# Weight buffers 128 bytes longer: all begin at the same address modulo 256 bytes

## The chip, the cores and the metric

One Trainium2 chip, one core of it. The metric is the device time of one execution in microseconds (us). The names used below for the engines are those of the profile: PE is TensorE's matmul, PEld its weight load, DVE VectorE, ACT ScalarE, POOL GpSimd, SP the queue that issues the weight transfers.

## The reference

A decoder trunk of two layers over 256 tokens of width 1024, in float32. Cut to what matters here:

```python
for l in range(DEPTH):                       # 2
    h = rms_norm(x, norm_mix_pre[l])
    proj = h @ w_in[l]                       # q, k, v, lru_x, lru_gate, glu, branch gates
    y_a = dilated_attention_mixer(q, k, v, cos, sin, w_o_attn[l])
    y_b = rg_lru_mixer(lru_x, lru_gate, ..., w_o_lru[l])
    y_c = conformer_conv_mixer(glu_in, ..., w_o_conv[l])
    merged = g0 * y_a + g1 * y_b + g2 * y_c  # g = sigmoid(gate_logits)
    x = x + rms_norm(merged @ w_out[l], norm_mix_post[l])
    h = rms_norm(x, norm_mlp_pre[l])
    u = square(relu(h @ w_mlp_up[l]))
    x = x + rms_norm(u @ w_mlp_down[l], norm_mlp_post[l])
```

## The kernel before

All weights come as a stream of 1 MB chunks (128 partitions x 2048 floats), 92 per layer, in an order written out by hand (`ORDER` and `chunk_plan`). `weights(l, name)` handles one chunk: SP loads it into `raw` (2 buffers), ACT casts it to a high part `whi` (fp32r), and DVE subtracts to get the low part `wlo`; both parts have 3 buffers, used in turn. A product of float32 accuracy is then three matmuls: high x high, high x low, low x high. A scheduler (`Sched`) fixes the order of each engine's instructions beforehand from costs by instruction size; it looks at the sizes of the reads and writes, not at the buffers' lengths.

There are two forms of chunk.

- In the *stationary* form (names lx, glu, lg, q, k, ga, gb, gc, ob, oa, oc, up) the weights are loaded into the array (PEld) and the activations `hh`/`hl` stream past, 256 columns a matmul. A chunk is 48 matmuls: 16 with `whi` (high and low activations in turn), 8 with `wlo`, and the same again. `up` comes in pairs of chunks, 96 matmuls.
- In the *moving* form (v, wo, ua, dn) the activations are loaded and the weights stream, 512 columns a matmul. A chunk is 24 matmuls: in each half 8 that take `whi` and `wlo` in turn, and then 4 with `whi` alone. `dn` comes in pairs, 48 matmuls. In the MLP the two kinds alternate: an `up` pair, a `dn` pair, and so on (the loop over `kb`).

Each of these matmuls has a weight load of its own, and PE goes from one to the next without a wait. What this text calls the *spacing* is the time from the start of one matmul to the start of the next.

The change is about where the buffers lie. A buffer of `whi` or `wlo` is `CHUNK + LINE // 4` floats long, 2080 x 4 = 8320 bytes in a partition, which is 32.5 x 256. The pool holds 2 x `raw` (8192 bytes each), 3 x `whi`, 3 x `wlo`, end to end. In the program of before, the first `whi` begins 128 bytes past a multiple of 256; so the three `whi` begin at 128, 0 and 128 modulo 256, and the three `wlo` at 0, 128 and 0. Of three chunks in a row two have high at 128 and low at 0, and the third the other way round (high at 0, low at 128). The `dn` and `up` chunks of the second layer go through them like this (1 and 2 are the buffers with high at 128, 3 is the one with high at 0):

```
dn pair (buffers)   up pair after it (buffers)
dn00 dn01 (3, 1)    up4  up5  (2, 3)
dn10 dn11 (1, 2)    up6  up7  (3, 1)
dn20 dn21 (2, 3)    up8  up9  (1, 2)
dn30 dn31 (3, 1)    up10 up11 (2, 3)      and so on, with period three
```

Reads of a stationary chunk begin 64 bytes into its buffer (`off = LINE // 8`), those of a moving chunk at its start (but v1 and v2). The activation buffers that these matmuls read begin at 128 modulo 256. One chunk of the first layer, `dn61`, is held in eight buffers of another pool (`HOLD`), all of which begin at 128. The LRU's own weights (`lwh`, `lwl`, whose matmuls are called psr and psi) also lie in that pool, without the 64 bytes.

Of the kernel before, what the change touches and what calls it, by code (L numbers as in the profile page):

```python
# [8 lines left out]
F32R = mybir.dt.float32r  # L9
# [4 lines left out]
P = 128  # L14
# [5 lines left out]
CHUNK = 2048  # L20
# [72 lines left out]
NHI = 3  # L93
# [10 lines left out]
LINE = 128  # L104
# [272 lines left out]
def trunk_kernel(ctx: ExitStack, tc: tile.TileContext, x_d, pos_d, w_d, lruw_d, par_d, gain_d, const_d, id_d, out_d):  # L377
    nc = tc.nc
    cp = ctx.enter_context(tc.tile_pool(name="cp", bufs=1))
    wp = ctx.enter_context(tc.tile_pool(name="wp", bufs=1))  # L380
    sp = ctx.enter_context(tc.tile_pool(name="sp", bufs=1))
    pp = ctx.enter_context(tc.tile_pool(name="pp", bufs=1, space=bass.MemoryType.PSUM))
    S = Sched()
# [4 lines left out]
    def slot(name, dt=F32, shape=(P, 2, T)):  # L388
        return S.buf(sp, shape, dt, "s2", name, NSLOT)
# [58 lines left out]
    def dma(eng, out, in_, nbytes):  # L448
        def fn():
            o = out.ap() if isinstance(out, View) else out  # L450
            i = in_.ap() if isinstance(in_, View) else in_
            eng.dma_start(out=o, in_=i)

        e = {id(nc.gpsimd): "POOL", id(nc.scalar): "ACT"}.get(id(eng), "SP")
        o = S.op(e, DMA_ISSUE[e], fn, views(in_), views(out))
        o.dma = nbytes / DMA_RATE / 1e3
        return o
# [40 lines left out]
    def split(hi, lo, src, scale=None):  # L498
        if scale is None:
            return act(hi, src, AF.Copy), tt(lo, src, hi.f32(), OP.subtract)  # L500
        return (act(hi, src, AF.Copy, scale=scale),
                stt(lo, src, scale, hi.f32(), OP.mult, OP.subtract))
# [5 lines left out]
    def weights(l, name, spread=False):  # L508
        c = CIDX[name]
        assert c == used[l], (name, c, used[l])  # L510
        used[l] += 1
        nm = f"{name}_{l}"
        raw = S.buf(wp, (P, CHUNK), F32, "raw", f"raw_{nm}", NRAW)
        if l or c:
            o = dma(nc.sync, raw.all(), w_d[l * NCH + c], CHUNK * P * 4)
            if l == 0 and c in late:
                S.follow(o, late[c])
        else:
            for s in range(2):
                o = dma(nc.sync, raw[:, s * HALF:(s + 1) * HALF], w_d[0][:, s * HALF:(s + 1) * HALF], HALF * P * 4)  # L520
                if ORDER[0][0] == "v":
                    S.follow(o, x1_load)
        if spread:
            hs, ls = [], []
            for q in range(4):
                hs.append(slot(f"whi_{nm}{q}", F32R, (P, 512)))
                ls.append(slot(f"wlo_{nm}{q}", F32R, (P, 512)))
                for o in split(hs[q].all(), ls[q].all(), raw[:, q * 512:(q + 1) * 512]):
                    o.prep = True
            return [(Quarters(hs[2 * s:2 * s + 2]), Quarters(ls[2 * s:2 * s + 2])) for s in range(2)]  # L530
        off = 0 if KIND[name] == "as" and name[:2] not in ("v1", "v2") else LINE // 8
        hi = Shifted(S.buf(wp, (P, CHUNK + LINE // 4), F32R, "whi", f"whi_{nm}", NHI), off)
        lo = Shifted(S.buf(wp, (P, CHUNK + LINE // 4), F32R, "wlo", f"wlo_{nm}", NHI), off)
        n = HALF if l == 0 and c < 2 else PREP
        for b in range(0, CHUNK, n):
            for o in split(hi[:, b:b + n], lo[:, b:b + n], raw[:, b:b + n]):
                o.prep = True
        return [(Part(hi, s * HALF), Part(lo, s * HALF)) for s in range(2)]
# [196 lines left out]
    for l in range(L):  # L735
# [49 lines left out]
        def glu(i):  # L785
            w = weights(l, f"glu{i}")
            ps = mm_ps(f"glu{i}_{l}")
            gemm(f"glu{i}", w, ps, hr)
            if i % 2 == 0:
                upad[i // 2] = S.buf(sp, (P, 2, 288), F32, "upad", f"upad{i}_{l}", 4)  # L790
                memset(upad[i // 2][:, :, 0:30], 0.0)
            u2 = upad[i // 2]
            th = slot(f"gth{i}_{l}", shape=(P, T))
            act(th.all(), ps[:, 1, :], AF.Tanh, scale=0.5)
            stt(u2[:, i % 2, 30:30 + T], th.all(), 1.0, ps[:, 0, :], OP.add, OP.mult)
            if i % 2 == 1:
                conv_pair(i // 2)
# [3 lines left out]
        def lx(j):  # L801
            w = weights(l, f"lx{j}")
            ps = mm_ps(f"lx{j}_{l}")
            gemm(f"lx{j}", w, ps, hr)
            xp = S.buf(sp, (P, 2, 260), F32, "xp", f"xp{j}_{l}", 2)
            memset(xp[:, :, 0:3], 0.0)
            act(xp[:, :, 3:3 + T], ps.all(), AF.Copy)
            u = slot(f"lu{j}_{l}")
            for s in range(2):
                i = 2 * j + s  # L810
                act(u[:, s, :], ps[:, s, :], AF.Identity, scale=p1(par, CW + 24 + i), bias=p1(par, CB + i))
            for k in range(3):
                for s in range(2):
                    i = 2 * j + s
                    stt(u[:, s, :], xp[:, s, k:k + T], p1(par, CW + k * 8 + i), u[:, s, :], OP.mult, OP.add)
            lu[j] = u
            luh[j] = slot(f"luh{j}_{l}", F32R)
            lul[j] = slot(f"lul{j}_{l}", F32R)
            split(luh[j].all(), lul[j].all(), u.all())
# [3 lines left out]
        def lg(j):  # L823
            w = weights(l, f"lg{j}")
            ps = mm_ps(f"lg{j}_{l}")
            gemm(f"lg{j}", w, ps, hr)
            q = slot(f"gq{j}_{l}")
            act(q.all(), ps.all(), AF.Square, scale=0.044715 ** 0.5)
            stt(q.all(), q.all(), 1.0, ps.all(), OP.add, OP.mult)
            act(q.all(), q.all(), AF.Tanh, scale=0.7978845608028654)  # L830
            g = slot(f"gel{j}_{l}")
            stt(g.all(), q.all(), 1.0, ps.all(), OP.add, OP.mult)
            gel[j] = g
# [319 lines left out]
        for t in range(2):  # L1153
            nm = f"pm{l}{t}"
# [79 lines left out]
        for t in range(2):  # L1234
            nm = f"pd{l}{t}"
# [100 lines left out]
```

## Time and profile before

| | us |
|---|---|
| three runs | 1129.45, 1129.23, 1126.79 (median 1129.23) |
| the profiled execution | 1128.12 |
| its span, first to last instruction | 1126.3 |
| PE busy in the span | 1101.3 |
| PEld busy | 1025.4 |
| DVE busy | 903.2 |
| ACT busy | 719.7 |

The profiled execution is the one that all rows are from. A row of the chain of waits is a stretch of the work that ended last: start, length, engine, and how many instructions in a row; length by count is the mean spacing. A row of the timeline has start, length, and the instruction; the difference of two starts is the spacing. The length of one matmul (0.28 or 0.39 us) contains its way through the array, overlaps with the next ones, and is not the spacing.

### The profile page before, as it was taken

How to read it: one execution, taken by the hardware profiler on the slowest of the kernel's cores; microseconds unless marked ns; L12 is line 12 of the kernel's file. 1: busy time of each engine (PE TensorE's matmuls, PEld its weight loads, DVE VectorE, ACT ScalarE, POOL GpSimd, SP SyncE). 2: the span in 40 equal slices, each digit the busy share in tenths (PEclk: the TensorE clock that was granted, in tenths of full speed). 3: DMA queues.
4: the chain of work that ended last, by engine and by line, in shares of the span. 5: the costliest groups of instructions: out<-in, count | busy, mean ns of one | idle time of the engine just before them, and what ended most of it. 6: DMA issues, size and time to landing. Idle time of an engine off the chain costs nothing.

```text
span 1126.3 us, 20586 instructions
## 1 busy us (share of the span) xinstructions
PE 1101.3 (98%) x8258; PEld 1025.4 (91%) x8258; DVE 903.2 (80%) x1374; ACT 719.7 (64%) x1173; POOL 76.4 (7%) x168
## 2 busy tenths in 40 slices
PE   7999999999999999999999999999999999999995
PEld 5999999999899899889889999999988988989984
DVE  6999999999879865555579999999995899555552
ACT  5879938687765554445569896569775756444441
POOL 1000022111000010000010000221200001000000
PEclk9999999999999999999999999999999999999998
DMA  8764366654345555555465643755624465555540
GB/s 290 246 207 151 147 229 221 212 179 134 149 170 190 201 209 189 190 184 190 182 225 187 207 159 141 252 191 197 205 96 163 153 239 189 192 184 189 199 174 38
DMA packets 37649, 209.76 MB, mean 186 GB/s; under 512 B 6449, under 2 KB 9777, under 8 KB 14130
## 3 DMA queue, kind: packets, MB, share of 16 engines
q1 hardware_dynamic: 32976, 200.05, 50.2%
q0 software_dynamic: 4576, 8.40, 2.3%
q8 instruction: 65, 1.06, 0.4%
q14 instruction: 30, 0.25, 0.1%
q10 hardware_dynamic: 2, 0.00, 0.0%
HBM read 201.08 MB, written 1.05 MB: 179 GB/s over the span
## 4 chain that ended last, share of the span: by engine, by line
PE 81%; DVE 7%; DMA 4%; ACT 4%; issue 1%; SPq 1%; POOL 0%; DVEq 0%; POOLq 0%; ACTq 0%
PE dn L476 15%; PE up L476 14%; PE glu L476 8%; PE v L476 5%; PE gc L476 4%; PE ga L476 4%; PE wo L476 4%; PE lx L476 4%; PE oc L476 4%; PE lg L476 4%; PE k L476 3%; PE ua L476 2%; PE oa L476 2%; PE ob L476 2%; PE pv L476 1%; PE tp L483 1%
## 5 line engine op out<-in xcount | busy, mean ns | idle before, releaser
L429 DVE TENSOR_TENSOR wlo_dn<-raw_dn,whi_dn 128x1024 fp32r<-128x1024 f32 (+1 forms) x66 | 75.8, 1189 | 68.6 <-ACT whi_dn L416 68.5
L416 ACT CAST whi_dn<-raw_dn 128x1024 fp32r<-128x1024 f32 (+1 forms) x66 | 64.4, 1022 | 75.8 <-PE dn L476 44.1
L433 DVE SCALAR_TENSOR_TENSOR c<-upad,parh,c 128x256 f32<-128x256 f32 x256 | 110.2, 476 | 0.1
L476 PE MATMUL up<-hh_mlp,whi_up 128*128 128x256 f32 x448 | 106.3, 278 | 0.0
L476 PE MATMUL up<-hl_mlp,whi_up 128*128 128x256 f32 x448 | 106.0, 278 | 0.0
L476 PE MATMUL dn<-wlo_dn,uh 128*128 128x512 f32 x256 | 100.5, 393 | 0.0
L476 PE MATMUL dn<-whi_dn,uh 128*128 128x512 f32 x256 | 100.4, 392 | 0.0
L429 DVE TENSOR_TENSOR wlo_up<-raw_up,whi_up 128x1024 fp32r<-128x1024 f32 x56 | 66.4, 1221 | 39.0 <-ACT whi_up L416 39.0
L423 ACT ACTIVATE cpd<-upad,parh 128x256 f32<-128x256 f32 x224 | 94.5, 500 | 4.1 <-DVE c L429 4.1
L476 PEld LDWEIGHTS up<-hl_mlp,whi_up 128*128 128x128 f32 x448 | 84.3, 188 | 0.6
L476 PEld LDWEIGHTS up<-hh_mlp,whi_up 128*128 128x128 f32 x448 | 84.2, 188 | 0.6
L416 ACT CAST whi_up<-raw_up 128x1024 fp32r<-128x1024 f32 x56 | 56.2, 1048 | 36.3 <-PE dn L476 20.0
L476 PE MATMUL dn<-whi_dn,ul 128*128 128x512 f32 x256 | 70.8, 392 | 0.0
L429 DVE TENSOR_TENSOR cpd<-cpd 128x1024 f32<-128x1024 f32 (+2 forms) x84 | 63.2, 772 | 0.9 <-ACT cpd L423 0.9
L476 PE MATMUL up<-hh_mlp,wlo_up 128*128 128x256 f32 x448 | 60.7, 278 | 0.0
L476 PE MATMUL glu<-hh_mix,whi_glu 128*128 128x256 f32 x256 | 59.6, 276 | 0.0
L476 PE MATMUL glu<-hl_mix,whi_glu 128*128 128x256 f32 x256 | 59.6, 276 | 0.0
L476 PEld LDWEIGHTS dn<-whi_dn,ul 128*128 128x128 f32 x256 | 48.0, 188 | 10.8
L476 PEld LDWEIGHTS dn<-wlo_dn,uh 128*128 128x128 f32 x256 | 48.0, 188 | 10.4
L476 PEld LDWEIGHTS dn<-whi_dn,uh 128*128 128x128 f32 x256 | 48.1, 188 | 10.3
L476 PEld LDWEIGHTS up<-hh_mlp,wlo_up 128*128 128x128 f32 x448 | 55.7, 188 | 0.0
L476 PEld LDWEIGHTS glu<-hh_mix,whi_glu 128*128 128x128 f32 x256 | 48.0, 188 | 0.0
(306 smaller groups left out, 3380.2 us busy)
## 6 DMA issues: line engine op xcount, KB each, us to landing
raw_dn<-w_in_stream SPq DMA_DIRECT2D x32, 1024.0 KB, 4.8
raw_up<-w_in_stream SPq DMA_DIRECT2D x28, 1024.0 KB, 4.8
raw_glu<-w_in_stream SPq DMA_DIRECT2D x16, 1024.0 KB, 4.9
raw_q<-w_in_stream SPq DMA_DIRECT2D x12, 1024.0 KB, 4.9
raw_k<-w_in_stream SPq DMA_DIRECT2D x12, 1024.0 KB, 4.8
raw_v<-w_in_stream SPq DMA_DIRECT2D x11, 1024.0 KB, 4.9
raw_lx<-w_in_stream SPq DMA_DIRECT2D x8, 1024.0 KB, 4.9
raw_lg<-w_in_stream SPq DMA_DIRECT2D x8, 1024.0 KB, 4.8
```

Of the source, the lines that this page charges most:

```text
L416: nc.scalar.copy(out.ap(), in_.ap())
L423: nc.scalar.activation(out.ap(), in_.ap(), func, scale=val(scale), **kw)
L429: lambda: nc.vector.tensor_tensor(out=out.ap(), in0=a.ap(), in1=b.ap(), op=op), [a, b], [out])
L433: lambda: nc.vector.scalar_tensor_tensor(out=out.ap(), in0=a.ap(), scalar=val(s), in1=b.ap(), op0=op0, op1=op1), [a, b] + views(s), [out])
L476: nc.tensor.matmul(out.ap(), lhsT=lhs.ap(), rhs=rhs.ap(), start=start, stop=stop)
L483: nc.tensor.transpose(out.ap(), a.ap(), ident.all().ap())
```

## The change

The two buffers become `CHUNK + LINE // 2` floats long, 2112 x 4 = 8448 bytes, which is 33 x 256. All three `whi` and all three `wlo` now begin at 128 modulo 256. What lies behind them in a partition moves by 6 x 128 = 768 bytes, three times 256. Instructions, their order, and the 64 bytes stay.

```diff
         off = 0 if KIND[name] == "as" and name[:2] not in ("v1", "v2") else LINE // 8
-        hi = Shifted(S.buf(wp, (P, CHUNK + LINE // 4), F32R, "whi", f"whi_{nm}", NHI), off)
-        lo = Shifted(S.buf(wp, (P, CHUNK + LINE // 4), F32R, "wlo", f"wlo_{nm}", NHI), off)
+        hi = Shifted(S.buf(wp, (P, CHUNK + LINE // 2), F32R, "whi", f"whi_{nm}", NHI), off)
+        lo = Shifted(S.buf(wp, (P, CHUNK + LINE // 2), F32R, "wlo", f"wlo_{nm}", NHI), off)
```

## Rows read from the trace of the kernel before

**Rows 1.** The page: span, PE, and the granted clock in 40 slices.

```profile
span 1126.3 us, 20586 instructions
...
PE 1101.3 (98%) x8258; PEld 1025.4 (91%) x8258; DVE 903.2 (80%) x1374; ACT 719.7 (64%) x1173; POOL 76.4 (7%) x168
...
PEclk9999999999999999999999999999999999999998
```

**Rows 2.** The chain of waits, MLP of the second layer: start, length, instructions.

```profile
959.80 11.06 PE dn L476 x48
970.86 10.90 PE up L476 x96
981.76 11.01 PE dn L476 x48
992.77 11.08 PE up L476 x96
...
1014.90 11.31 PE up L476 x96
...
1092.64 22.15 PE dn L476 x96
```

**Rows 3.** Timeline of PE, end of dn41 (buffer 2), up12 (buffer 3).

```profile
1057.67 0.39 PE L476 MATMUL dn<-whi_dn,uh 128*128 128x512 f32 x1
...
1058.13 1.07 PE L476 MATMUL dn<-whi_dn,ul 128*128 128x512 f32 x4
1059.03 0.28 PE L476 MATMUL up<-hh_mlp,whi_up 128*128 128x256 f32 x1
1059.15 0.28 PE L476 MATMUL up<-hl_mlp,whi_up 128*128 128x256 f32 x1
```

**Rows 4.** Timeline of PE, the held chunk dn61, second use.

```profile
554.10 0.39 PE L476 MATMUL dn<-whi_dn,uh 128*128 128x512 f32 x1
...
555.49 0.39 PE L476 MATMUL dn<-whi_dn,uh 128*128 128x512 f32 x1
...
556.85 0.40 PE L476 MATMUL dn<-whi_dn,uh 128*128 128x512 f32 x1
```

**Rows 5.** Timeline of PE, end of dn01 (buffer 1), up4 (buffer 2).

```profile
969.78 1.09 PE L476 MATMUL dn<-whi_dn,ul 128*128 128x512 f32 x4
970.70 0.28 PE L476 MATMUL up<-hh_mlp,whi_up 128*128 128x256 f32 x1
970.83 0.28 PE L476 MATMUL up<-hl_mlp,whi_up 128*128 128x256 f32 x1
970.94 0.28 PE L476 MATMUL up<-hh_mlp,whi_up 128*128 128x256 f32 x1
```

**Rows 6.** Timeline of PE, end of dn21 (buffer 3), up8 (buffer 1).

```profile
1013.82 1.09 PE L476 MATMUL dn<-whi_dn,ul 128*128 128x512 f32 x4
1014.74 0.28 PE L476 MATMUL up<-hh_mlp,whi_up 128*128 128x256 f32 x1
```

**Rows 7.** The chain of waits, both layers' lx, glu and lg.

```profile
30.83 27.20 PE glu L476 x240
...
63.47 16.32 PE glu L476 x144
79.79 10.88 PE lx L476 x96
94.99 10.88 PE lg L476 x96
107.31 10.27 PE lg L476 x88
...
647.19 11.31 PE lg L476 x96
```

**Rows 8.** Busy time by window, 117 to 201 us: each engine, clock, DMA.

```profile
117.00:201.00 84.00, 81.62 (x714) 80.40 (x714) 80.44 (x118) 57.23 (x94) 11.98 (x25) 1.00 0.58 198
```

**Rows 9.** The instructions that write wlo_up: duration ns min/median/max.

```profile
L429 DVE TENSOR_TENSOR wlo_up<-raw_up,whi_up x56: 1211/1220/1226, 387.5 to 1078.1; 128x1024 fp32r<-128x1024 f32 x56
```

## The prediction

> **What bounds the kernel now.** The page comes first: PE is busy 1101.3 of 1126.3 us, and its granted clock is at the upper level, 2.4 GHz, in practically every slice [rows 1]. So the time is a number of matmuls times their spacing, and the question is whether the spacing depends on where a buffer begins.
>
> The chain of waits answers that, because it counts matmuls in a row. 240 glu matmuls take 27.20 us, 113.3 ns each, and the second run of 144 has the same 113.3 [rows 7]. But `up`, with the same instructions on the same shapes, takes 10.90, 11.08 or 11.31 us for 96: 113.5, 115.4 and 117.8 ns [rows 2]. The first layer has the same three lengths for its `up` pairs, twice each, in another order. There are thus two spacings in the stationary form, a short one of 113.3 and a long one of 117.8, and 11.08 is a pair that changes from one to the other. `lg` shows both as well: 10.88 for 96 in the first layer, 11.31 in the second [rows 7]. Nobody waits in these stretches. The three lengths of `up` go with the three positions in the ring of buffers: buffers (2, 3) give 10.90, (3, 1) give 11.08, (1, 2) give 11.31. This is what the change touches.
>
> The moving form is finer. A `dn` pair takes 11.06 or 11.01 us for 48, 230.4 and 229.4 ns [rows 2]. Just before up12, two matmuls that take the high buffer at 128 and the low one at 0 last 0.46 us together, 230 ns each; then four in a row from the buffer at 128 last 0.90, about 226 each [rows 3]. In the held chunk, where everything begins at 128, the first six matmuls last 1.39 us, 231.7 each, and the next six 1.36, 226.7 [rows 4]: with all at 128 the spacing settles on its short value within six matmuls and stays.
>
> **The change part by part.**
>
> *Moving form (dn, wo).* After the change every weight read of dn and wo begins at 128, as in the held chunk. I take six matmuls at 231.7 and the rest at 226.7: a dn pair is then 6 x 0.2317 + 42 x 0.2267 = 10.91 us, against 11.06 (two pairs of three) and 11.01 (one of three). In a layer the six pairs dn0 to dn5 gain 4 x 0.15 + 2 x 0.10 = 0.80, and the last 96 matmuls go from 22.15 to 21.79, 0.36 [rows 2]. That is 1.16 for 384 matmuls, 3.0 ns each; with the 192 of wo at the same rate, 960 x 3.0 = 2.9 us less over both layers. Bounds: 0.2267 for all of them from the first matmul gives 3.3; if the spacing stays at 231.7, dn loses some 1.3 us. ua and the two v chunks of this form at 128 are cut up by transposes: nothing.
>
> *Stationary form: up.* Here all weight reads move to the offset that buffers 1 and 2 have for high parts now (128 + 64 = 192). Two things decide: with which spacing an `up` pair begins, and whether it changes on the way.
>
> For the second, a pair in buffers (1, 2) holds the long spacing over all 96 matmuls (11.31), though its reads alternate between offsets; the way back to the short one is seen only in pairs that use buffer 3, where the high part lies at 0 and the low one at 128 [rows 2]. After the change no buffer lies so. A long spacing will stay long, and a short one short.
>
> For the first, the end of the preceding dn pair matters. There are three cases now. After dn01, whose last four matmuls still have the slow spacing of 230 ns (0.92 for four), up4 has one spacing of 0.13 and is then short [rows 5]. After dn21 (last buffer with high at 0; 0.92 for four) up8 is long from the start [rows 6, 2]. After dn41 (last buffer with high at 128, dn settled at 226 ns) up12 is long from the first matmul on: 0.12 us [rows 3]. After the change every dn pair ends as dn41 does, settled at 226.7. What differs from up12 is only the offset of up's own reads, 192 in place of 64. The two offsets are alike once the spacing is short: glu goes through all three buffers at 113.3 [rows 7]. I therefore take the entry of up12: long.
>
> Then all twelve uninterrupted `up` pairs of both layers take 11.31. Now they sum to 4 x (10.90 + 11.08 + 11.31) = 133.16; 12 x 11.31 = 135.72. Cost: +2.6 us. The bound on the other side is the short spacing for all, 12 x 96 x 0.1133 = 130.5: -2.6. The first pair of each layer is interrupted by transposes and counts 0.
>
> *Stationary form: lx and glu.* They follow v0, a moving chunk, which will end settled like dn. Twelve chunks (240 + 144 + 96 matmuls of rows 7 and two more chunks of 48) run one after the other, 576 a layer, short now. Entered long and with no way back, they cost 576 x (117.8 - 113.3) = 2.6 us a layer, +5.2 in both. Bounds: 0 and 5.2.
>
> *lg.* It follows psr and psi. In the second layer lg enters buffers (1, 2) from them long (11.31), in the first layer buffer 3 short (10.88) [rows 7]. With all offsets as in (1, 2) I take it long: 10.88 to 11.31 and 10.27 to 88 x 0.1178 = 10.37, +0.5. The second layer is long already: 0. Bounds: -0.6 and +0.6.
>
> *From 117 to 201 us, and the same stretch of the second layer*: PE is busy 81.62 of 84.00 us [rows 8], the rest it waits for rotary and LRU work of DVE, ACT and their transfers. A change of spacing is covered by those 2.4 us: 0. Without that cover 14 chunks, 672 matmuls, would cost up to 3.0 a layer.
>
> *From 201 to 360 us* (ga, gc, k, oa, oc between score matmuls and transposes) both spacings occur and every interruption starts anew. I take 0; all long or all short is about 1.5 us a layer either way.
>
> *The writers.* DVE's subtraction into `wlo` takes 1211 to 1226 ns in all 56 chunks of `up`, which went through all three buffers [rows 9]. So the begin of a buffer costs the writers nothing, and no transfer moves: SP loads `raw`, which stays. The 768 bytes by which other pools move are three times 256; the trace shows no dependence on more than that, and I count 0.
>
> *Sum.* -2.9 + 2.6 + 5.2 + 0.5 = +5.4 us. The sum is made on the profiled execution, 1128.12 us; its median over three runs is 1.1 higher, 1129.23. That gives 1134.6 us.
>
> **A rule against it.** By the rows, PE's spacing differs by 4% between buffers while its clock, form and shape are the same [rows 2]. The Trainium skill, page "TensorE: Matmul & The Clock Gate", section "Step-by-step: what each phase is for", says that PE has two independent SBUF read ports, and that loading the next weights takes no read bandwidth from the running matmul. By that rule alone the addresses could not matter, and the change would give 1129.2; the trace disagrees already before the change, in 10.90 against 11.31 us.
>
> **The rivals.**
>
> *The short spacing on entry (faster).* Place: the first matmuls of up and lx after a settled moving chunk. Reads at 192 after a moving chunk from 128 are short within three matmuls after dn01 [rows 5]; the only long entry after a settled dn is at offset 64 [rows 3]. If 192 is what makes the difference, up is short in all pairs (-2.6), lx and glu stay as they are (0), dn and wo give -2.9, lg +0.5: -5.0, 1124.2 us. Against it: up8 at offset 192 enters long and holds it [rows 6, 2]. It decides as soon as the first `up` pair after a dn pair is below 10.95 us.
>
> *Nothing that can be measured.* Either the two spacings come from how the kinds of matmul follow one another and not from the addresses, so that the change does not do what it is about, and long stretches move about without a change of their share; or up turns long and dn short while glu keeps 113.3, which is -2.9 + 2.6 + 0.5 = +0.2. Then 1129.2 to 1129.4. For it: glu, lx and the first lg pair of the first layer keep 113.3 ns [rows 7] although they cross all three buffers. Against the first of these: up's lengths repeat with the period of the ring.
>
> **How the numbers follow.** A measurement here tells about 0.3% from no change, 3.4 us. Forecast (long entry, held): 0.50; its own range is 1131.5 to 1137.5, from glu long in one layer only to 201-360 us long as well. Faster rival: 0.27, 1122.5 to 1125.5. Nothing: 0.23. The range 1123.5 to 1137.5 leaves out the outer part of both, less than 2 in 10. Slower by over 0.3%: 0.49; within: 0.25; faster: 0.26.
>
> **What will show it.** In the chain of waits: dn pairs at 10.9 us for 48 (step one); all up pairs of one length, 11.31 if the entry is long, 10.88 if it is short (step two); 27.20 or 28.27 us for the 240 glu matmuls (step three); lg at 11.31 in both layers. The prediction fails if the long spacing finds a way back with all reads at one offset, or if a settled dn hands over short; it fails on dn if its pairs stay at 11.06.

## The result and the profile after

The changed kernel takes 1134.72 us, median of four runs (1134.37 to 1136.28); the kernel before, run beside it, 1128.64. The ratio is 1.0052, interval 1.0031 to 1.0073: slower by 3.5 to 8.2 us, with 1134.6 forecast. The profiled execution of the changed kernel took 1134.92 us, its span 1133.2: 6.9 more than before.

The page after, to be held against [rows 1]:

```profile
span 1133.2 us, 20586 instructions
...
PE 1112.2 (98%) x8258; PEld 1040.2 (92%) x8258; DVE 904.4 (80%) x1374; ACT 720.8 (64%) x1173; POOL 76.2 (7%) x168
...
PEclk9999999999999999999999999999999999999998
```

The same 8258 matmuls, the same granted clock, but PE is busy 10.9 us longer (and its weight loads 14.8); DVE and ACT gain about 1 us each. The time in which PE does nothing falls from 25.0 to 21.0 us, so PE does not wait longer; its matmuls stand further apart, and a part of that fills what were waits. Where, the chain of waits of the changed kernel says (start, length, instructions in a row), against [rows 2] and [rows 7]:

```profile
24.40 5.66 PE lx L476 x48
30.05 28.27 PE glu L476 x240
...
63.98 16.96 PE glu L476 x144
...
341.61 22.61 PE oc L476 x192
...
364.23 20.43 PE wo L476 x90
...
399.21 2.83 PE up L476 x24
402.48 8.18 PE up L476 x72
...
652.90 11.31 PE lg L476 x96
...
798.60 11.31 PE k L476 x96
...
898.33 21.76 PE oc L476 x192
...
966.52 10.90 PE dn L476 x48
977.42 11.31 PE up L476 x96
...
1099.80 21.80 PE dn L476 x96
```

Read as spacings: 240 glu matmuls at 28.27 us are 117.8 ns (113.3 before), the 144 at 16.96 the same; each of the twelve uninterrupted `up` pairs takes 11.31; each `dn` pair 10.90 or 10.91, 227 ns. The three lengths of `up` and the two of `dn` have become one each.

Two of these rows show that 192 is not the long spacing by itself. oc takes 22.61 us in the first layer and 21.76 in the second, 117.8 and 113.3 ns, with all its reads at 192 both times. And the first `up` pair, which transposes interrupt, is long in its first 24 matmuls (2.83 us) and short in the 72 behind the transposes (8.18).

### The profile page after: what moved, and what is told of

Read it like the earlier page. It is cut to its first block, busy times and chain, and to the rows that moved or that the text cites. A ratio compares the mean times of both kernels' runs of the same rounds, so it can differ in the third digit from the quotient of the medians.

```text
span 1133.2 us, 20586 instructions
## 1 busy us (share of the span) xinstructions
PE 1112.2 (98%) x8258; PEld 1040.2 (92%) x8258; DVE 904.4 (80%) x1374; ACT 720.8 (64%) x1173; POOL 76.2 (7%) x168
## 4 chain that ended last, share of the span: by engine, by line
PE 92%; DMA 3%; ACT 1%; DVE 1%; SPq 1%; issue 1%; POOL 0%; DVEq 0%; POOLq 0%; ACTq 0%
PE dn L476 15%; PE up L476 14%; PE glu L476 8%; PE k L476 6%; PE v L476 5%; PE q L476 4%; PE gc L476 4%; PE ga L476 4%; PE lg L476 4%; PE lx L476 4%; PE oc L476 4%; PE wo L476 4%; PE gb L476 3%; PE ob L476 3%; PE oa L476 2%; PE ua L476 2%
## 5 line engine op out<-in xcount | busy, mean ns | idle before, releaser
L476 PEld LDWEIGHTS glu<-hl_mix,whi_glu 128*128 128x128 f32 x256 | 48.5, 189 | 0.0
```

Of the source, the lines that this page charges most:

```text
L476: nc.tensor.matmul(out.ap(), lhsT=lhs.ap(), rhs=rhs.ap(), start=start, stop=stop)
```

## The experiments

All are built on the program before or after; none leaves work out. A stationary read begins at the buffer's 128 plus four times the second pair of offsets, a moving read at 128 plus four times the first, modulo 256: an offset of 0 floats is 128, 16 is 192, 32 is 0, 48 is 64. "Moving" here means v0, wo, ua and `dn`; v1 and v2 follow the stationary offsets. The buffers of all but the first kernel have the changed length.

| stationary high, low | moving | us | ratio to before, 95% |
|---|---|---|---|
| as before, rest moved by 768 bytes | as before | 1128.7 | 0.9987 to 1.0011 |
| 192, 192 (the change) | 128 | 1134.72 | 1.0031 to 1.0073 |
| 192, 192 | alternating, as before | 1134.12 | 1.0030 to 1.0063 |
| alternating, as before | 128 | 1127.96 | 0.9981 to 1.0009 |
| 64, 192 | 128 | 1124.97 | 0.9942 to 0.9975 |
| 192, 64 | 128 | 1133.95 | 1.0028 to 1.0057 |
| 0, 0 | 128 | 1148.68 | 1.0158 to 1.0199 |
| 128, 128 | 128 | 1151.62 | 1.0183 to 1.0224 |
| 64, 64 | 0 | 1143.74 | 1.0096 to 1.0157 |
| 64, 192 | 192 | 1124.94 | 0.9951 to 0.9984 |
| 64, 192, order high, high, low | 128 | 1121.08 | 0.9910 to 0.9953 |
| 192, 192, same order | 128 | 1137.19 | 1.0053 to 1.0092 |
| 192, 64, same order | 128 | 1124.68 | 0.9951 to 0.9976 |

**Only the 768 bytes.**

```diff
+    memset(S.buf(sp, (P, 192), F32, "pad", "pad", 1, False)[:, 0:1], 0.0)
```

> The kernel before with one spare tile of 768 bytes ahead of the pool behind the weight buffers: all other tiles move as far as the change moved them, the weight buffers stay where they were. Mine (the weight reads' own begin modulo 256 sets the spacing): nothing moves; dn pairs of the second layer stay at 11.01 to 11.06 us, up pairs at 10.90, 11.08 and 11.31, glu at 27.20 for 240; 1128 to 1130 us. Rival (the 768 bytes by which everything else moved did it): up pairs all at 11.31, glu at 28.27; about 1134.7 us.

Measured 1128.7 us, and the chain has the old lengths:

```profile
972.67 10.89 PE up L476 x96
...
994.57 11.08 PE up L476 x96
...
1016.71 11.31 PE up L476 x96
```

The shift of the other pools is worth nothing: what acts is where the weight reads begin.

**The two halves of the change, one at a time.** First stationary reads all at 192 as in the change, with moving reads at the old alternation:

```diff
+        third = ring[0] % 3 == 2
+        ring[0] += 1
-        off = 0 if KIND[name] == "as" and name[:2] not in ("v1", "v2") else LINE // 8
+        off = ((32, 0) if third else (0, 32)) if KIND[name] == "as" and name[:2] not in ("v1", "v2") else (16, 16)
```

> The changed buffers, stationary reads all at 192 modulo 256 as in the change; but the moving reads alternate between 128 and 0 from chunk to chunk of the ring as they did before. Mine (it is the settled end of the moving chunk that makes the next stationary chunk long): dn pairs at 11.01 to 11.06 as before, glu at 27.20 for 240, up by its place in the ring, 10.90 where the dn before it does not settle and 11.31 where it does; about 1129.5 us. Rival (one constant offset of the stationary reads is by itself the long spacing): up 11.31 in all pairs, glu 28.27, and no gain on dn: about 1137.5 us.

Measured 1134.12: the time that I expected was missed by 4.6 us. The chain:

```profile
30.78 28.27 PE glu L476 x240
...
587.58 27.20 PE glu L476 x240
...
975.84 10.89 PE up L476 x96
986.73 11.01 PE dn L476 x48
997.74 11.31 PE up L476 x96
...
1020.11 11.31 PE up L476 x96
```

`dn` and `up` came with the ring's period, as I expected. But the pair at 1020.11 is long behind a `dn` pair that does not settle (its last chunk has high at 0), and glu was long in the first layer and short in the second, after a v0 that does not settle in either. After an unsettled moving chunk the entry can thus go both ways, and I had taken it for short. The rival falls too: reads at 192 throughout can be short (27.20, 10.89). What they lack is a way back, which the 11.31 behind the 11.01 shows: before, the pair at that place of the ring took 11.08 [rows 2]. Of the time, 2.5 us went into lx and glu of the first layer, about 1 into the two MLPs, and 1.6 into the stretch from ob (201.99 before, 204.55 now) to wo (360.76 and 364.88), which I had counted at nothing.

Then the other half, moving reads all at 128, stationary reads alternating as before (`third` as above):

```diff
+        off = (0, 0) if KIND[name] == "as" and name[:2] not in ("v1", "v2") else (48, 16) if third else (16, 48)
```

> The changed buffers, moving reads all at 128 modulo 256 as in the change; the stationary reads alternate as before (two chunks of three with high at 192 and low at 64, the third the other way round). Mine (the entry is long after every settled dn, and the third chunk's high at 64, low at 192 brings it back): dn 10.91, up about 10.95 to 11.1 where the pair contains the third chunk, 11.31 where it does not; glu back to short within its first three chunks, 27.2 to 27.6 for 240; about 1127 us. Rival (nothing brings a long spacing back once dn hands over settled): as the change, about 1134.7 us.

Measured 1127.96. The chain:

```profile
582.86 27.48 PE glu L476 x240
...
970.56 11.17 PE up L476 x96
...
992.63 11.08 PE up L476 x96
...
1014.62 11.31 PE up L476 x96
```

The moving chunks settle (10.90 to 10.94 us a `dn` pair), every pair enters long, and a chunk with high at 64 and low at 192 brings it back: in the second half of the pair (11.17), at the end of its first chunk (11.08), or not at all where the pair has no such chunk (11.31). What `dn` gains, `up` loses. By the medians the moving half is worth -0.7 us, within the interval of nothing, and the stationary half +5.5; the loss is the stationary half's, because it takes the way back away.

**High at 64, low at 192 in every buffer.**

```diff
+        off = (0, 0) if KIND[name] == "as" and name[:2] not in ("v1", "v2") else (48, 16)
```

> The changed buffers, but the reads of a stationary chunk begin at 64 modulo 256 in the high part and at 192 in the low part, in every buffer; moving reads at 128 as in the change. This is the one combination with which a long spacing went back to the short one before. Mine (a long spacing ends where high at 64 hands over to low at 192): dn stays at 10.91 a pair, each up pair enters long and is short again within its first chunk, 10.93 to 11.15 us, and holds that; glu 27.20 to 27.4 for 240; about 1125 us, faster than both kernels. Rival (after a settled dn the long spacing holds whatever the offsets of the stationary reads): up 11.31, glu 28.27, about 1134.7 us.

Measured 1124.97, 0.42% faster than before. The chain, and the timeline of PE in up4, behind a settled dn01:

```profile
24.72 5.63 PE lx L476 x48
30.36 27.20 PE glu L476 x240
...
970.83 11.08 PE up L476 x96
```

```profile
972.55 1.11 PE L476 MATMUL up<-hh_mlp,wlo_up 128*128 128x256 f32 x8
973.50 0.28 PE L476 MATMUL up<-hh_mlp,whi_up 128*128 128x256 f32 x1
...
975.38 1.09 PE L476 MATMUL up<-hh_mlp,wlo_up 128*128 128x256 f32 x8
976.30 0.28 PE L476 MATMUL up<-hh_mlp,whi_up 128*128 128x256 f32 x1
```

From the first row to the second are eight low matmuls in 0.95 us, still long; from the third to the fourth eight in 0.92, and all that follow are 113.3 apart. Each pair is long until its second handoff from high to low, some 41 matmuls, and then short. The first handoff does not do it here. It is no rule: the pairs of 11.17 us in the kernel before this one are 64 long matmuls and 32 short ones, and there the pair's first handoff from high at 64 to low at 192 ended it.

**The mirror image, 192 and 64.**

```diff
+        off = (0, 0) if KIND[name] == "as" and name[:2] not in ("v1", "v2") else (16, 48)
```

> The mirror image of the kernel with high at 64 and low at 192: high parts of stationary chunks are read at 192 modulo 256, low parts at 64, in every buffer; moving reads at 128. Mine (only a handoff from high at 64 to low at 192 ends a long spacing; the other direction does not): up pairs 11.31 us, glu 28.27 for 240, dn 10.91: about 1134.7 us, as the change. Rival (any change of offset between the high and the low part ends it): up 11.08, glu 27.20: about 1125 us, as with 64 and 192.

Measured 1133.95, and the chain stays long:

```profile
975.90 11.31 PE up L476 x96
```

All twelve pairs are like this one. In blocks of 16 high and 8 low, that a read changes its offset is not enough.

**Other constant offsets.** Stationary reads at 0, and then without the 64 bytes, at 128:

```diff
+        off = (0, 0) if KIND[name] == "as" and name[:2] not in ("v1", "v2") else (32, 32)
```

> The changed buffers, but every stationary read begins at 0 modulo 256, in the high and in the low part; moving reads at 128. Mine (one constant offset has no way back, whichever it is): up pairs 11.31, glu 28.27 for 240, about 1134.7 us. Rival (what matters is where the weight load begins in relation to the activations at 128: half of 256 apart they do not disturb each other): up 10.88, glu 27.20, about 1123 us.

```diff
+        off = (0, 0) if KIND[name] == "as" and name[:2] not in ("v1", "v2") else (0, 0)
```

> The changed buffers without the 64 bytes of the stationary chunks: every weight read, stationary and moving, begins at 128 modulo 256, as the activations do. Mine: a constant offset has no way back, and psr and psi, which read at 128 already, are spaced 120 ns in the trace; so up at 11.3 to 11.5 us a pair and glu at 28.3 to 28.8: 1135 to 1141 us. Rival (only reads at 64 or 192 are ever long): up 10.88, glu 27.20, about 1123 us.

Measured 1148.68 and 1151.62, far beyond both expectations. The chain at 0, then at 128:

```profile
31.01 28.80 PE glu L476 x240
...
335.71 11.39 PE oa L476 x96
...
990.66 11.53 PE up L476 x96
```

```profile
31.32 28.80 PE glu L476 x240
...
992.62 11.51 PE up L476 x96
```

28.80 us for 240 is 120.0 ns: a third spacing, and none shorter in the glu chunks and the uninterrupted `up` pairs. At 0 I had expected 117.8. The cost is not limited to these: at 128 every stationary chunk is at 120.0, and at 0 several others are at 118.7 (oa, 11.39 for 96). With 0, the stretch from ob to wo of the first layer alone grows by 3.9 us (201.99 to 360.76 before, 207.19 to 369.89 now), and I had priced only `up` and glu.

**All alike, but at 64 and 0.**

```diff
+        off = (32, 32) if KIND[name] == "as" and name[:2] not in ("v1", "v2") else (48, 48)
```

> All buffers alike as in the change, but at another place: moving reads all begin at 0 modulo 256, stationary ones all at 64. Mine (the moving form settles because its reads begin at 128, not because they are all alike): dn pairs stay at 11.0 to 11.1 us, up pairs enter as they may and hold what they enter with, 11.31 for most, glu 28.27 in at least one layer: 1134 to 1138 us. Rival (being alike is what settles it): dn 10.91, up 11.31, glu 28.27: about 1134.7 us; dn tells them apart, not the time.

Measured 1143.74; the time is 6 us above what I expected, and where they went was not traced, while `dn` decides as I expected:

```profile
973.88 11.15 PE dn L476 x48
985.02 11.31 PE up L476 x96
```

At 11.14 to 11.16 us a pair, 232 ns, moving reads at 0 do not settle. That all begin at the same place is not what makes `dn` fast; beginning at 128 is.

**Moving reads at 192.**

```diff
+        off = (16, 16) if KIND[name] == "as" and name[:2] not in ("v1", "v2") else (48, 16)
```

> The kernel with stationary high at 64 and low at 192, but the moving reads begin at 192 modulo 256 in place of 128. Mine (moving reads settle at 226.7 ns only where they begin at 128, as the activations that are loaded with them do): dn pairs at 11.0 to 11.15 us, up 10.88 to 11.1: 1127 to 1133 us. Rival (every begin but 0 is as good as 128): dn 10.90, up 11.08: about 1125 us.

Measured 1124.94. The chain:

```profile
957.26 10.99 PE dn L476 x48
968.25 11.08 PE up L476 x96
```

`dn` takes 10.99 a pair, 229 ns: between 0 (232) and 128 (227). For `dn` that is at the lower end of what I expected, and in all it is 2 us better. The 960 matmuls of `dn` and wo should cost 2 us more than at 128, but the medians show no loss (1124.94 against 1124.97); what makes up for it was not separated.

**The order within a chunk.** On the kernel with 64 and 192, `up`, glu and lx take high, high, low in turn in place of 16 high and 8 low; the same products are summed in another order.

```diff
+            if mix:
+                c = [x for k in range(8) for x in (a[2 * k], a[2 * k + 1], b[k])]
+                a, b = c[:16], c[16:]
```

> The kernel with high at 64 and low at 192, and in up, glu and lx the 24 matmuls of a half chunk take the parts in the order high, high, low, high, high, low in place of 16 high and then 8 low: the same products, summed in another order. There each up pair was long for 40 to 42 matmuls, until the second handoff from high to low, and took 11.08 us. Mine (the handoff from 64 to 192 is what ends the long spacing): handoffs now come every third matmul, the long spacing ends within the first 12, up pairs 10.90 to 10.95 us: 2 us less than there, about 1123 us. Rival (a row of reads at 192, not one handoff, is needed, or the spacing ends after some 40 matmuls whatever their order): up 11.08 to 11.31, 1125 us or more.

Measured 1121.08, the fastest of all: 0.69% below before (0.47 to 0.90). The chain, and PE's timeline where up4 begins:

```profile
965.15 10.89 PE up L476 x96
```

```profile
964.99 0.28 PE L476 MATMUL up<-hh_mlp,whi_up 128*128 128x256 f32 x1
965.10 0.28 PE L476 MATMUL up<-hl_mlp,whi_up 128*128 128x256 f32 x1
965.22 0.28 PE L476 MATMUL up<-hh_mlp,wlo_up 128*128 128x256 f32 x1
965.33 0.28 PE L476 MATMUL up<-hh_mlp,whi_up 128*128 128x256 f32 x1
```

The step from the second to the fourth row is 0.23 us for two, from 115 down to 113.3: the long spacing ends at the first or second handoff after the entry, and all twelve pairs take 10.89, glu 27.20 for 240. The profiled execution gained 6.8 us on the one with 64 and 192: 2.6 in the two MLPs, 0.4 in lx, 0.5 in the second layer's oa and oc, and 3.0 between lg and oa or k, where the handoffs of the other chunks were not changed. Why that last part is shorter was not separated; the medians differ by 3.9.

Two more kernels ask whether it is the order or the offsets. The same order with all at 192:

```diff
+        off = (0, 0) if KIND[name] == "as" and name[:2] not in ("v1", "v2") else (16, 16)
```

> The changed buffers with the order high, high, low of the fast kernel, but its stationary reads all at 192 modulo 256 as in the change. Mine (it is the handoff from high at 64 to low at 192 that ends a long spacing): long holds, up pairs 11.31 us, glu 28.27 for 240: about 1134 us. Rival (the order high, high, low is by itself the cure): up 10.89, glu 27.20: about 1121 us.

Measured 1137.19, and the chain is that of the change:

```profile
977.72 11.31 PE up L476 x96
```

The order alone cures nothing (glu 28.27 for 240). And with the mirror image, high at 192 and low at 64:

```diff
+        off = (0, 0) if KIND[name] == "as" and name[:2] not in ("v1", "v2") else (16, 48)
```

> The same order with the offsets exchanged: high at 192, low at 64; a chunk then has handoffs from 64 to 192 as well, but from a low part to the next high one. Mine (only from high to low does it end a long spacing, as with 16 and 8 in a row): up pairs 11.31 us, glu 28.27: about 1134 us. Rival (any handoff from 64 to 192 or back does, if it comes often): up 10.9, about 1121 us.

Measured 1124.68. The chain, and the timeline at up4:

```profile
969.76 10.90 PE up L476 x96
```

```profile
969.84 0.28 PE L476 MATMUL up<-hh_mlp,wlo_up 128*128 128x256 f32 x1
969.96 0.28 PE L476 MATMUL up<-hh_mlp,whi_up 128*128 128x256 f32 x1
970.07 0.28 PE L476 MATMUL up<-hl_mlp,whi_up 128*128 128x256 f32 x1
970.19 0.28 PE L476 MATMUL up<-hh_mlp,wlo_up 128*128 128x256 f32 x1
970.30 0.28 PE L476 MATMUL up<-hh_mlp,whi_up 128*128 128x256 f32 x1
```

The first row is the pair's third matmul; the steps are 0.12, 0.11, 0.12 and 0.11, and the pair's 10.90 us leave room for a handful of long ones. The rival held for `up`, and my theory of one direction fell: with a change of offset every one or two matmuls the long spacing does not last, either way round. Whether such a change also ends one that has long been held, neither kernel shows. The time did not follow the rival: 3.6 us above the 1121.08 of the other way round, and of the 4.7 us between the two profiled executions 4.4 lie between lg and oa of the two layers, where the chunks keep their blocks of 16 and 8.

In blocks only high at 64 to low at 192 ended it. In a row without an interruption no long spacing ended under one constant offset, nor with high at 192 and low at 64 in blocks. An interruption by other matmuls does end it at times, as in the first `up` pair of the changed kernel. Which change takes effect, and after how many handoffs, stays open.

## Why the prediction was right

**What bounds the kernel** was right: PE's spacing, at one clock and with no more waiting. The Trainium skill, page "TensorE: Matmul & The Clock Gate", section "Step-by-step: what each phase is for", says that loading takes no read bandwidth from the running matmul. Read as a rule on the spacing, the runs disagree, with 113.3, 117.8 and 120.0 ns for the same matmuls and loads, and the measurement decides.

**dn and wo** settled as said: pairs at 10.90 to 10.91 for 10.91 forecast. The twelve pairs gained 1.73 us, the rest of `dn` 0.50, the 180 wo matmuls on the chain 0.57: 2.8 against 2.9. The kernels with moving reads at 0 and 192 show that of the three places it is 128 that settles them.

**The entry of up.** I took up12's: long. All twelve pairs entered long and took 11.31, +2.56 us against +2.6. The rival of a short entry at 192 is out: in the seven kernels with moving reads at 128 and stationary ones at 64 or 192, all twelve pairs and both lx enter long, 98 times out of 98.

**No way back.** With a constant offset the long spacing held to the end of each uninterrupted row, here, at 192 in the other order, and at 64. Over an interruption it did not have to: the first `up` pair of each layer went from long to short at 192 behind its transposes. I had counted the interrupted stretches at nothing. My reason was too narrow, too: I had the one arrangement that the trace showed, high before low with 64 before 192, and with the offset changing every one or two matmuls the other way round is short as well.

**lx and glu**: 5.03 us measured (65.37 to 67.85 in the first layer, 65.29 to 67.84 in the second), 5.2 forecast. **lg**: 0.7 against 0.5. I had read the second layer as long already, but its second pair before, 10.18 us for 88, was long in its first half only.

**The stretches that I counted at nothing** are where the sum was off. The cover from 117 to 201 us held: lg0 starts 2.00 us later, the last ob pair 2.16, and PE idles 0.8 of 84 us where it idled 2.4. In the second layer it did not quite: from 670 to 775 us 0.65 were added. From ob to wo 1.3 us came in the first layer, 0.4 in the second, with k at 11.31 in both, oc at 22.61 for 192 in the first (21.76 before) and the v1 pair, of which the sum says nothing, at 11.19 for 48 (11.09 before); that lies in the 1.5 a layer that I had named as the bound. Against these 2.4 us stands that the profiled execution began lx 0.9 earlier than before (24.40 for 25.30). So the span grew by 6.9 where the sum said 5.4; the medians differ by 6.1. That the forecast of 1134.6 lies 0.1 from the median is in part luck: the sum was 0.7 short, and the median that it was set on 0.6 higher than that of the runs beside the change.

**The writers and the transfers**: DVE's subtraction into `wlo_up` takes 1212 to 1227 ns after the change (1211 to 1226 in [rows 9]; these are 56 instructions, two for each of 28 chunks, not 56 chunks), and the 768 bytes did nothing, as said.

## What to carry to other kernels

Where PE is busy 98% of the time and its clock is steady, count matmuls in a row in the chain of waits and compare the spacing of like shapes; one that varies with the ring of buffers may be a matter of addresses, and was worth 4 to 6% of the matmul time here. Making all buffers alike is no remedy by itself: it fixes one state for all, and here that was the long one. Try the offsets of the loaded and of the streamed operand separately, and look for the arrangement that ends a bad state, not only for one that is good while it lasts; here 64 and 192 in turn within the chunk, at 1121.08 us, beat both the kernel before and the changed one.

## What the runs showed of the hardware that was not expected

- The begin of the loaded weights modulo 256 bytes sets the spacing of 128x256 matmuls whose streamed activations begin at 128: 120.0 ns at 128, 120.0 or 118.7 at 0, 113.3 or 117.8 at 64 and 192. The 64 bytes that the kernel before puts in front of its stationary reads are worth some 17 us of 1134.72 (1151.62 without them).
- In the 128x512 matmuls of `dn` and wo the streamed weights count: 227 ns a matmul when they begin at 128, 229 at 192, 232 at 0, with loaded activations at 128 throughout. It does not carry over to v1 and v2, which load every second token: 233 ns with weights at 128 as at 192 (11.18 and 11.19 us for 48), 230 with high at 64 and low at 192 (11.04). Why 128 is the best place for `dn` and the worst for loaded weights, these runs do not tell.
- At 64 and 192 the spacing has memory. The same instructions at the same addresses run at 113.3 or 117.8 ns for hundreds of matmuls, depending on what came before. Behind a moving chunk that had settled at 128 the first matmuls were long in all 98 cases; in an uninterrupted row a short spacing never turned long.
